# Splitting the last 16 partitions of eight stores over fewer DMA engines, and a SyncE program without a loop, in a batched matmul

## The chip, the cores and the metric

The kernel runs on one core of a Trainium2 chip. The metric is the device time of one execution, in microseconds (us); less is better. The core has the engines TensorE (PE, with its weight loads PEld), VectorE (DVE), ScalarE (ACT), GpSimd (POOL) and SyncE (SP), and 16 DMA engines that move data between the chip's main memory (DRAM) and the on-chip memory (SBUF, 128 partitions). In this kernel SyncE issues all data transfers; its own queue is written SPq in the profile.

## What is computed

```python
b1, b2, m, k, n = 8, 16, 256, 512, 384
# x: (b1, b2, m, k) float32, weight: (b1, b2, k, n) float32
return np.matmul(x, weight).astype(np.float32)
```

These are 128 independent products of a 256x512 by a 512x384 matrix, all in float32 in DRAM. The inputs are 168 MB and the output 50 MB.

## The kernel before

Four matrices form a group (G = 4), so there are NG = 32 groups. In each, a partition holds R = 8 rows of x, of 512 elements (16,384 bytes in a row of memory), and later 8 rows of the output, of 384 elements (12,288 bytes). A group is loaded with one transfer of x and two of the weights, cast to bfloat16, transposed and multiplied on TensorE, copied out of PSUM, and stored with one transfer.

The part of SyncE: loads run LAG = 4 groups ahead of stores. A load waits until the buffer it fills was cast (x_cast, w_cast); a store waits until ScalarE copied the results (o_copied).

```python
def load(e, t, U, s):
    n = t * U + s
    if not isinstance(n, int) or n >= XS:                 # XS = 2 buffers for x
        e.wait_ge(x_cast, n + (1 - XS))
    e.dma_start(x_sb[s % XS][:], x_rows[...]).then_inc(x_in[s % XS], 16)
    for d in range(G // D):                               # two halves of the weights
        slot = (s * (G // D) + d) % WS                    # WS = 4 buffers
        if not isinstance(n, int) or n >= 2:
            e.wait_ge(w_cast, n * (G * S) + ((d + 1) * D * S - 2 * G * S))
        e.dma_start(w_sb[slot][:], w_rows[...]).then_inc(w_in[slot], 16)

def store(e, t, U, s, pieces=1):
    n = t * U + s
    dram = o_rows[bass.ds(n * (G * M), G * M)].rearrange("(p r) n -> p r n", r=R)
    for q in range(pieces):
        rows = slice(q * R // pieces, (q + 1) * R // pieces)
        e.wait_ge(o_copied, n * T + ((q + 1) * T // pieces + BIAS))
        e.dma_start(out=dram[:, rows], in_=out_sb[s % OS][:, rows]).then_inc(
            o_out[s % OS], 16)

@block.sync
def _(e):
    U = OS                                                # OS = 4 output buffers
    for n in range(LAG):
        load(e, 0, NG, n)
    rounds = (NG - LAG) // U
    with e.Fori(0, rounds) as t:
        for s in range(U):
            load(e, t, U, LAG + s)
            store(e, t, U, s)
    for n in range(rounds * U, NG):
        if n + LAG < NG:
            load(e, 0, NG, n + LAG)
        store(e, 0, NG, n, T if n == NG - 1 else 1)       # the last store in T = 4 pieces
    ...                                                   # waits for the last stores
```

The part of ScalarE that a store's completion holds up: before it fills an output buffer again it waits until the store of four groups earlier has landed.

```python
def copy_out(e, t, U, s, q):
    n = t * U + s
    if q == 0:
        e.wait_ge(o_out[s % OS], (t * (U // OS) + s // OS) * 16 + 16)
    e.wait_ge(p_made, n * T + (q + 1 + BIAS))
    e.copy(out=out_sb[s % OS][:, 2 * q : 2 * q + 2, :],
           in_=po[(s * T + q) % PO][:, :, :N]).then_inc(o_copied, 1)
```

Of the kernel before, what the change touches and what calls it, by code (L numbers as in the profile page):

```python
# [11 lines left out]
def kernel(  # L12
# [7 lines left out]
    P = 128  # L20

    b1, b2, M, K = x.shape
    _, _, _, N = weight.shape
    B = b1 * b2
    KO = K // P
# [3 lines left out]
    o_rows = out.rearrange("b1 b2 m n -> (b1 b2 m) n")  # L29
# [9 lines left out]
    G = 4  # L39
    C = P // G  # L40
    R = G * M // P
    T = R // 2
# [3 lines left out]
    NG = B // G  # L46

    XS, WS, OS = 2, 2 * G // D, 4
# [2 lines left out]

    LAG = 4

    ctx.enter_context(tc.tile_critical())  # L54

    def sbuf(name, shape, dtype, n):
        return [
            ctx.enter_context(nc.sbuf_tensor(f"{name}{s}", shape, dtype)) for s in range(n)
        ]
# [6 lines left out]
    def sems(name, n):  # L66
        return [tc.alloc_semaphore(f"{name}{s}") for s in range(n)]
# [9 lines left out]
    out_sb = sbuf("out_sb", [P, R, N], fp32, OS)  # L77
# [6 lines left out]
    id_done, x_cast, w_cast, t_made, t_copied, p_made, o_copied = (  # L84
        sems(name, 1)[0]
        for name in (
            "id_done", "x_cast", "w_cast", "t_made", "t_copied", "p_made", "o_copied"
        )
    )
    x_in, w_in, o_out = sems("x_in", XS), sems("w_in", WS), sems("o_out", OS)  # L90


    BIAS = 8


    def load(e, t, U, s):
        n = t * U + s
        if not isinstance(n, int) or n >= XS:
            e.wait_ge(x_cast, n + (1 - XS))
        e.dma_start(  # L100
            x_sb[s % XS][:],
            x_rows[bass.ds(n * (G * M), G * M)].rearrange("(p r) k -> p r k", r=R),
        ).then_inc(x_in[s % XS], 16)
        for d in range(G // D):
            slot = (s * (G // D) + d) % WS
            if not isinstance(n, int) or n >= 2:
                e.wait_ge(w_cast, n * (G * S) + ((d + 1) * D * S - 2 * G * S))  # L107
            e.dma_start(  # L108
                w_sb[slot][:],
                w_rows[bass.ds(n * (G * K) + d * (D * K), D * K)].rearrange(  # L110
                    "(p k) n -> p k n", k=S * KO
                ),
            ).then_inc(w_in[slot], 16)

    def store(e, t, U, s, pieces=1):
        n = t * U + s
# [5 lines that stand above are left out]
                o_out[s % OS], 16  # L122
            )

    def cast_x(e, t, U, s):
        n = t * U + s
        e.wait_ge(x_in[s % XS], (t * (U // XS) + s // XS) * 16 + 16)
        e.wait_ge(t_made, n * T + ((1 - BS) * T + BIAS))
        for h in range(S):
            ins = e.copy(  # L130
                out=x_bf[s % BS][:, :, h],
                in_=x_sb[s % XS][:].rearrange("p r (q s c) -> p r s q c", s=S, c=KO)[
                    :, :, h
                ],
            )
        ins.then_inc(x_cast, 1)
# [65 lines left out]
    @block.gpsimd  # L202
    def _(e):
        e.memset(identity[:], 0.0).then_inc(id_done, 1)  # L204
        e.wait_ge(id_done, 1)
        make_identity(nc, identity[:], nomemset=True)
        e.drain().then_inc(id_done, 1)

    @block.sync
    def _(e):  # L210
        U = OS
        for n in range(LAG):
            load(e, 0, NG, n)
        rounds = (NG - LAG) // U
        with e.Fori(0, rounds) as t:
            for s in range(U):
                load(e, t, U, LAG + s)
                store(e, t, U, s)
        for n in range(rounds * U, NG):
            if n + LAG < NG:  # L220
                load(e, 0, NG, n + LAG)
            store(e, 0, NG, n, T if n == NG - 1 else 1)
        for s in range(OS):
            e.wait_ge(o_out[s], 16 + 16 * (NG // OS + (T - 1 if s == (NG - 1) % OS else 0)))

    @block.vector
    def _(e):
# [65 lines left out]
```

## Time and profile before

| what | value |
|---|---|
| time, median of 2 runs | 519.82 us (519.78 to 519.85) |
| profiled run | 520.11 us, span in the trace 518.3 us |
| busy: PE, PEld | 315.5 us (61%), 198.8 us (38%) |
| busy: DVE, ACT | 323.9 us (62%), 212.7 us (41%) |
| busy: DMA queue of the data, share of 16 engines | 99.2% |
| bytes read, written | 167.77 MB, 50.33 MB |

A share of busy time says how full an engine is over the whole span, not whether it sets the end. The row of DMA shares in 40 slices says the same by time: each digit is a slice, in tenths. A transfer over 128 partitions is carried out as packets, one for each partition here, spread over the 16 DMA engines; each engine ends its part with a small write of 4 bytes that counts the semaphore up by one. So the trace holds 16 completions for each transfer, and the transfer has landed with the last of them. A packet's record has a start, a duration and a size, but not the number of its DMA engine.

### The profile page before, as it was taken

Reading aid. Unit: us, or ns where it says so; the run is one execution under the profiler, and the core shown is the slowest. Engines: PE = TensorE matmul, PEld = TensorE weight load, DVE = VectorE, ACT = ScalarE, POOL = GpSimd, SP = SyncE. Lnnn points to the kernel's source line nnn. Section 1 sums busy time; section 2 is a strip of 40 time slices with the busy share of each in tenths; the row PEclk is TensorE's granted clock in tenths of the full one; section 3 lists DMA queues with packets and bytes.
Section 4 is the critical chain, followed back from the end, with each engine's and each line's share of the span. In section 5 each row is a group of like instructions: output and inputs, shape, how many; then the busy total and the mean of one; then the engine's idle time right before and its main releaser. Section 6 shows DMA issues by size and latency. Waiting matters only on the chain.

```text
span 518.3 us, 11239 instructions
## 1 busy us (share of the span) xinstructions
PE 315.5 (61%) x4608; PEld 198.8 (38%) x4608; DVE 323.9 (62%) x384; ACT 212.7 (41%) x193; POOL 0.7 (0%) x6
## 2 busy tenths in 40 slices
PE   0686773576655675655756557665567665675653
PEld 0455452343433443433424334343344333443331
DVE  0878867655577555775556765557755577555670
ACT  3065462454234553245542445423454324553242
POOL 0000000000000000000000000000000000000000
PEclk9988788877687778678776877778787868886787
DMA  8999999999999999999999999999999999999995
GB/s 332 431 426 426 427 427 429 430 426 429 430 428 429 431 426 428 428 431 431 425 429 429 430 430 429 427 428 429 430 430 428 426 431 430 429 428 427 428 431 214
DMA packets 18868, 218.16 MB, mean 421 GB/s; under 512 B 2096, under 2 KB 2096, under 8 KB 2608
## 3 DMA queue, kind: packets, MB, share of 16 engines
q1 hardware_dynamic: 18864, 218.11, 99.2%
q8 instruction: 2, 0.03, 0.0%
q14 instruction: 2, 0.02, 0.0%
HBM read 167.77 MB, written 50.33 MB: 421 GB/s over the span
## 4 chain that ended last, share of the span: by engine, by line
DMA 81%; DVE 12%; issue 2%; PE 2%; ACT 1%; SPq 0%; DVEq 0%; ACTq 0%
DMA w_sb<-in_weight_dram 81%; DVE w_bf L148 12%; PE po L181 2%; ACT x_bf L130 0%; DVEq _compat.py:109 0%; SPq L108 0%; ACT out_sb L195 0%; SPq L100 0%; DVE x_t L154 0%; DVEq L143 0%; DVEq L230 0%; SPq L107 0%; ACTq L194 0%; SPq L288 0%; SPq L54 0%
## 5 line engine op out<-in xcount | busy, mean ns | idle before, releaser
L148 DVE CAST w_bf<-w_sb 64x1536 bf16<-64x1536 f32 x256 | 244.5, 955 | 179.4 <-DMA w_sb<-in_weight_dram 166.7
L181 PE MATMUL po<-w_bf,x_t 128*32 128x384 bf16 x4096 | 231.4, 400 | 121.0 <-DVE x_t L154 121.0
L195 ACT COPY out_sb<-po 128x768 f32<-128x768 f32 x128 | 99.2, 802 | 290.2 <-PE po L181 290.2
L181 PEld LDWEIGHTS po<-w_bf,x_t 128*32 128x32 bf16 x4096 | 124.5, 117 | 225.4 <-DVE x_t L154 130.9
L167 PE MATMUL pt<-identity,x_bf 128*128 128x128 f32 x512 | 84.0, 329 | 73.0 <-ACT x_bf L130 73.0
L130 ACT CAST x_bf<-x_sb 128x2048 bf16<-128x2048 f32 x64 | 118.4, 1901 | 6.1 <-DMA x_sb<-in_x_dram 6.1
L167 PEld LDWEIGHTS pt<-identity,x_bf 128*128 128x128 f32 x512 | 74.3, 213 | 84.9 <-issue 84.9
L154 DVE COPY x_t<-pt 128x1024 bf16<-128x1024 bf16 x128 | 79.5, 683 | 1.0
L130 ACT ACT_TABLE_LOAD x1 | 1.3, 1283 | 1.3 <-PEq L237 1.3
masks.py:199 POOL TENSOR_SCALAR_AFFINE_SELECT identity<-identity 128x128 f32<-128x128 f32 x1 | 0.3, 292 | 0.2 <-POOL identity L204 0.2
L204 POOL MEMSET identity<- 128x128 f32 x1 | 0.2, 204 | 0.5 <-SPq L54 0.5
L277 POOL MEMSET const-bfloat16-1.0<- 128x1 bf16 x1 | 0.1, 101 | 0.0
L277 POOL MEMSET const-uint8-127<- 128x1 uint8 x1 | 0.1, 101 | 0.0
L277 POOL MEMSET const-float32-0.0<- 128x1 f32 x1 | 0.1, 98 | 0.2 <-issue 0.2
L277 POOL MEMSET const-float32-1.0<- 128x1 f32 x1 | 0.1, 98 | 0.0
## 6 DMA issues: line engine op xcount, KB each, us to landing
w_sb<-in_weight_dram SPq DMA_DIRECT2D x64, 1536.0 KB, 27.5
x_sb<-in_x_dram SPq DMA_DIRECT2D x32, 2048.0 KB, 25.8
out_dram<-out_sb SPq DMA_DIRECT2D x31, 1536.0 KB, 30.6
out_dram<-out_sb SPq DMA_DIRECT2D x4, 384.0 KB, 3.6
```

The lines of the kernel that those rows point to most:

```text
L130: ins = e.copy(out=x_bf[s % BS][:, :, h], in_=x_sb[s % XS][:].rearrange("p r (q s c) -> p r s q c", s=S, c=KO)[:, :, h],)
L148: e.tensor_copy(out=w_bf[(s * G + d * D + a) % WBS][h * HP : (h + 1) * HP], in_=w_sb[slot][a * HP : (a + 1) * HP, h * KO : (h + 1) * KO, : ...
L154: e.tensor_copy(out=x_t[s % TS][:, 2 * q : 2 * q + 2], in_=pt[(s * T + q) % PT][:].bitcast(bf16),).then_inc(t_copied, 1)
L167: ins = e.transpose(pt[(s * T + q) % PT][:, rr, h, :], words[:, 2 * q + rr, h :: KO // 2], identity[:],)
L181: ins = e.matmul(po[(s * T + q) % PO][mine, rr, :N], x_t[s % TS][:, 2 * q + rr, ko // 2, mine, ko % 2], w_bf[(s * G + i) % WBS][:, ko, :], ...
L195: e.copy(out=out_sb[s % OS][:, 2 * q : 2 * q + 2, :], in_=po[(s * T + q) % PO][:, :, :N],).then_inc(o_copied, 1)
L204: e.memset(identity[:], 0.0).then_inc(id_done, 1)
L277: nc = _bacc.Bacc("TRN2", target_bir_lowering=False, num_devices=1)
```

## The change

SyncE's loop over groups is written out, so that each group can be treated by itself. For eight of the 32 groups (4, 7, 10 ... 25) the store is cut into three transfers: partitions 0 to 111, then k partitions from 112 on, then the 16 - k left. The numbers k are 15, 14 ... 8. The intent is to give the 16 DMA engines unequal numbers of packets: a transfer of k partitions is to use the first k engines, so that the last engines get fewer packets and the first ones more. The three transfers count a semaphore of their own (few); one step later SyncE waits for it and then counts up o_out, for which ScalarE waits.

```diff
+    FEW = {4: 15, 7: 14, 10: 13, 13: 12, 16: 11, 19: 10, 22: 9, 25: 8}
...
+    few = sems("few", 1)[0]
...
+    def store_few(e, n, k):
+        dram = o_rows[n * G * M : (n + 1) * G * M].rearrange("(p r) n -> p r n", r=R)
+        e.wait_ge(o_copied, n * T + (T + BIAS))
+        for a, b in ((0, P - 16), (P - 16, P - 16 + k), (P - 16 + k, P)):
+            e.dma_start(out=dram[a:b], in_=out_sb[n % OS][a:b]).then_inc(few, 16)
...
     @block.sync
     def _(e):
-        U = OS
+        done = [16] * OS
         for n in range(LAG):
             load(e, 0, NG, n)
-        rounds = (NG - LAG) // U
-        with e.Fori(0, rounds) as t:
-            for s in range(U):
-                load(e, t, U, LAG + s)
-                store(e, t, U, s)
-        for n in range(rounds * U, NG):
+        for n in range(NG):
             if n + LAG < NG:
                 load(e, 0, NG, n + LAG)
-            store(e, 0, NG, n, T if n == NG - 1 else 1)
+            if n in FEW:
+                store_few(e, n, FEW[n])
+            else:
+                store(e, 0, NG, n, T if n == NG - 1 else 1)
+            if n - 1 in FEW:
+                e.wait_ge(few, 48 * (1 + list(FEW).index(n - 1)))
+                e.sem_inc(o_out[(n - 1) % OS], 16)
+            done[n % OS] += 16 * T if n == NG - 1 else 16
         for s in range(OS):
-            e.wait_ge(o_out[s], 16 + 16 * (NG // OS + (T - 1 if s == (NG - 1) % OS else 0)))
+            e.wait_ge(o_out[s], done[s])
```

## The prediction

> **What bounds the kernel now.** I read the page's slices and DMA queues first, then the chain that ended last, then SyncE's own waits, and last the single packets of the trace.
>
> ```profile
> DMA  8999999999999999999999999999999999999995
> GB/s 332 431 426 426 427 427 429 430 426 429 430 428 429 431 426 428 428 431 431 425 429 429 430 430 429 427 428 429 430 430 428 426 431 430 429 428 427 428 431 214
> ...
> q1 hardware_dynamic: 18864, 218.11, 99.2%
> ...
> DMA 81%; DVE 12%; issue 2%; PE 2%; ACT 1%; SPq 0%; DVEq 0%; ACTq 0%
> ...
> w_sb<-in_weight_dram SPq DMA_DIRECT2D x64, 1536.0 KB, 27.5
> x_sb<-in_x_dram SPq DMA_DIRECT2D x32, 2048.0 KB, 25.8
> out_dram<-out_sb SPq DMA_DIRECT2D x31, 1536.0 KB, 30.6
> ```
>
> The DMA engines are busy in every slice but the first and last, at a flat 425 to 431 GB/s, and the chain is 81% weight loads. A transfer takes 26 to 31 us from issue to landing, though each engine works on its share of it for only some 4 or 5 us: the queue is always about two groups deep. SyncE's waits show that it is early, not late:
>
> ```profile
> SPq L100 <- ACT x_bf L130: 257.1, 30, 9.4
> SPq L108 <- DVE w_bf L148: 138.1, 58, 3.6
> SPq L121 <- ACT out_sb L195: 36.9, 6, 15.9
> ```
>
> It waits 9 us per group for a buffer of x and 2.4 us for each buffer of weights, with the queue full behind it. So only the work of the DMA engines counts, and of them only the one that ends last.
>
> **The packets.** In mid-run one engine's packet of 12,288 bytes follows the last after about 0.459 us (mean duration 0.462, starts 3 to 4 ns before the end of the one before), and one of 16,384 after 0.608 us. A group gives each engine 8 of x, 16 of weights and 8 of output: 8 x 0.608 + 24 x 0.459 = 15.9 us, and 32 groups make 508 us. That is the kernel; latency at the start and a tail make the rest. Sorting the 16 completions of the last weight load by time, and subtracting the first, gives how far each engine lags behind the fastest (us): 0, 0.28, 0.28, 0.32, 0.32, 0.43, 0.46, 0.53, 0.59, 0.64, 0.65, 0.76, 1.04, 1.93, 2.36, 4.18. Their mean is 0.92. At the first load the largest lag was 0.88. Two engines jump by over 1 us by the fourth load, at 28 and 38 us, where the trace has two packets of instruction fetch of 16,384 bytes (1.06 and 1.11 us). The slowest drifts: its packets take some 3.4 ns more each, and a fetch at 91 us hits it. It ends at 516.3 us of the span; twelve others end near 512.2, for they wait for the last piece of the output, copied at 510.3. So **the ceiling** for any levelling is 4.18 - 0.92 = 3.3 us, 0.6%.
>
> [...]
>
> **The change part by part.**
>
> 1. *Loop to straight code.* It removes register arithmetic and branches from SyncE, which has about 9 us to spare per group: worth 0. It adds code: some 32 x 8 instructions instead of a third of them, at most one or two more fetch packets. Each cost one engine 0.3 to 1.1 us in the trace, and only counts if it hits the engine that ends last: 0 to +0.5 us.
>
> 2. *Packets moved between engines.* An engine has 8 packets in a normal store. In a cut one it has 7 from the 112 partitions, one more if its number is below k, and one more if it is below 16 - k. Summed over k = 15 ... 8, engine 15 loses 8 packets, engine 14 loses 7, ... engine 8 loses 1; engine 0 gains 8, engine 1 gains 7, ... engine 7 gains 1. In time engine 15 loses 8 x 0.459 = 3.7 us and engine 0 gains 3.7. If the drifting engine is 15, as the shape of the change suggests, its lag goes from 4.2 to 0.5. But then engine 0 is last. The fastest engine unhindered would end at 493.3 (its completion of the last weight load) + 4 stores x 8 x 0.459 + 32 small packets x 0.118 = 511.8. With 3.7 more and its own lag of 0 to 1.04 it ends between 515.4 and 516.5, against 516.3 now: -0.9 to +0.2 us. If engine 0 is one of the two that lag by 1.9 and 2.4, +1.1 to +1.5; engine 1 (+3.2 us) and 2 (+2.8) have the same risk, smaller. The ramp moves as much onto one end as it takes off the other: expected **-0.2 us**, not -3.3.
>
> 3. *The new wait on SyncE.* It comes after the next store's issue, and ends when the cut store has landed. Issue to landing is 30.6 us and a step 15.9, so SyncE stands some 14 us, where the next load of x would have been issued after about 9. The load is issued some 6 us late. When the cut store has landed on the last engine, one whole group, 15.9 us of packets less the lag between engines, is still queued behind it; so no engine runs dry: 0. ScalarE needs that buffer only three steps after, so the forwarded count is in time: 0.
>
> 4. *Two more transfers per cut store.* Two more issues of about 0.35 us each on SyncE, hidden, and up to two 4-byte packets of 9 ns per engine: 16 x 9 ns = 0.14 us: +0.1.
>
> 5. *Shared SBUF ports.* This is the part on which I am unsure. [...] It isn't given back: the engines have no idle time. That would be 524 to 532 us.
>
> **Rivals.**
>
> - *Levelling works and the ports don't bind* (4 in 10): parts 1, 2 and 4 alone, about 519.0 to 521.3. For it: the ports' limit is nowhere seen in this trace. Against a larger gain: engine 0.
> - *Port sharing* (6 in 10): 521 to 533. For it: [...] nothing in the queue has slack. Against: the order in which 112 partitions are dealt to 16 engines isn't known to me, and engines that once waited are out of step later and collide less.
> - *SyncE becomes late*, the queue runs dry in each cut step. It would cost several us each time; the depth of the queue and 9 us of waits speak against it. I give it one in twenty, within the second's range.
> - *The last k engines aren't those thought*, and the drifting engine is among those that gain: +0.5 to +3.7 us, thus 520 to 523.5.
>
> **Range and chances.** The two main cases centre on 519.8 and 527; between them I put **523.0 us**. The low end 518.8 is the levelling with a lucky engine 0; the high end 532 is port sharing at its estimate's end. Faster by over 2% (under 509.4) lies below what the packets need, 0.01. Slower by over 2% (over 530.2) needs the upper third of the port case: 0.20. The rest, 0.79, is within 2%.
>
> **What would show it.** The lags of the 16 completions at the last weight load: under levelling alone the largest is 3.5 to 4.5, under port sharing 8 or more, and its jumps stand at the eight cut stores. Packets of 12,288 bytes longer than 0.6 us there, in hundreds, are ports; none means that part 5 fails. SyncE's wait for few should be some 14 us each, with the DMA row still at 9. More instruction fetches would show part 1. I am wrong altogether if the time falls under 518, which would mean that the engines that gain packets had idle time I didn't see, or if it passes 533, which would mean dry queues.

## The result, and the profile after

The changed kernel takes 524.99 us (median of 2 runs, 524.94 to 525.04), the kernel before 519.82: a ratio of 1.010, 95% interval 1.0056 to 1.0143. It is slower by 5.2 us. The forecast was 523.0 with a range of 518.8 to 532.0.

Of the page after, the rows by slice, the packets and queue, the two lines of the chain, and the issues with their time to landing:

```profile
DMA  8999999999999999999999999999999999999994
GB/s 338 429 425 428 425 430 428 427 432 422 401 424 431 421 407 427 430 409 421 429 429 426 430 433 428 426 428 429 424 431 429 431 427 432 428 428 428 427 391 192
DMA packets 18996, 218.16 MB, mean 417 GB/s; under 512 B 2224, under 2 KB 2224, under 8 KB 2736
...
q1 hardware_dynamic: 18992, 218.11, 98.8%
q8 instruction: 2, 0.03, 0.0%
q14 instruction: 2, 0.02, 0.0%
...
DMA 79%; DVE 10%; issue 5%; PE 2%; SPq 1%; ACT 1%; DVEq 0%; ACTq 0%
DMA w_sb<-in_weight_dram 62%; DMA out_dram<-out_sb 18%; DVE w_bf L158 10%; PE po L191 2%; ACT x_bf L140 0%; SPq L123 0%; SPq L103 0%; DVEq _compat.py:109 0%; SPq L111 0%; ACT out_sb L205 0%; DVE x_t L164 0%; DVEq L153 0%; SPq L233 0%; DVEq L242 0%; ACTq L138 0%
...
w_sb<-in_weight_dram SPq DMA_DIRECT2D x64, 1536.0 KB, 27.5
x_sb<-in_x_dram SPq DMA_DIRECT2D x32, 2048.0 KB, 25.5
out_dram<-out_sb SPq DMA_DIRECT2D x23, 1536.0 KB, 30.9
```

The bytes are the same. There are 128 more packets, all small: the semaphore counts of the cut pieces, 16 more per cut store. Each cut store has 32 completions from DMA engines where a whole one has 16: 16 for the first piece, then k and 16 - k. The DMA row is still at 9 everywhere but at the ends. What is new stands in the row below it: three slices fall to 401, 407 and 409 GB/s. A slice is 13.1 us, so these lie at 131 to 144, 183 to 196 and 222 to 235 us, where the first three cut stores (groups 4, 7 and 10), or the loads just behind them, reach the DMA engines. A packet that waits is counted as busy, so the share hides what the rate shows: at 128 to 136 us it is 1.01 before and 1.02 after, at 433 and 403 GB/s. Five stretches of 8 us at places of cut stores, with the columns start and end, length, PE, PEld, DVE, ACT and POOL busy, clock, DMA share and GB/s, first before and then after:

```profile
128.00:136.00 8.00, 3.35 (x28) 2.63 (x32) 7.78 (x10) 2.02 (x3) 0.00 (x0) 0.64 1.01 433
176.00:184.00 8.00, 3.53 (x32) 2.65 (x36) 7.78 (x10) 1.71 (x3) 0.00 (x0) 0.63 1.00 429
224.00:232.00 8.00, 3.71 (x32) 2.83 (x36) 7.78 (x11) 1.59 (x3) 0.00 (x0) 0.61 1.01 431
320.00:328.00 8.00, 3.96 (x32) 2.96 (x36) 7.78 (x11) 1.31 (x2) 0.00 (x0) 0.59 1.01 430
464.00:472.00 8.00, 3.80 (x35) 2.75 (x38) 7.81 (x10) 0.85 (x2) 0.00 (x0) 0.55 1.00 429
```

```profile
128.00:136.00 8.00, 3.68 (x32) 2.82 (x36) 7.78 (x10) 1.71 (x3) 0.00 (x0) 0.62 1.02 403
176.00:184.00 8.00, 3.05 (x40) 2.29 (x28) 7.64 (x8) 3.99 (x4) 0.00 (x0) 1.00 1.00 405
224.00:232.00 8.00, 4.80 (x64) 3.50 (x52) 5.73 (x6) 5.11 (x5) 0.00 (x0) 0.81 1.00 389
320.00:328.00 8.00, 5.85 (x92) 3.90 (x84) 5.04 (x6) 5.80 (x5) 0.00 (x0) 0.93 1.01 424
464.00:472.00 8.00, 5.47 (x92) 3.85 (x84) 5.05 (x6) 5.81 (x5) 0.00 (x0) 0.97 1.02 433
```

The DMA share is 1.00 to 1.02 in all ten lines; the rate falls clearly at the first three cut stores, and hardly at the later two. (The other columns shift because the same clock time meets another point of the group's cycle.)

The single packets say what happens inside. Before, 3 packets of 12,288 bytes after the start took over 0.6 us; after, 105, of which 85 start between 120 and 250 us. At the first cut store the 112-partition part runs almost clean, at 0.46 us a packet with a few of 0.6 to 0.9. Then the 15 partitions come, each on another engine (the store has 16 + 15 + 1 = 32 completions), within 0.2 us, and among these packets stand durations of 0.57, 0.60, 0.83, 1.34, 1.43, 1.80 and 2.24 us.

The completions of the last weight load show what it costs. Before, the fastest engine completes it at 493.33 us of the span, the mean at 494.25 and the slowest at 497.50. After, it is 490.72, 497.04 and 503.02. So the mean engine lost 2.8 us, which no moving of packets between engines can do, and the slowest lost 5.5. The other 2.7 us are uneven sharing. The spread grew from 4.2 to 12.3 us.

SyncE's waits after:

```profile
SPq L103 <- ACT x_bf L140: 182.7, 22, 9.7
SPq L233 <- DMA out_dram<-out_sb: 119.3, 8, 15.9
SPq L111 <- DVE w_bf L158: 115.6, 43, 4.3
SPq L131 <- ACT out_sb L205: 37.3, 6, 16.4
```

The new wait (L233) is 14.9 us for each cut store, as forecast, and the chain now runs 18% through stores. That looks like a culprit, so it was tested.

### The profile page after: what moved, and what is told of

Read it like the earlier page. It is cut to its first block, busy times and chain, and to the rows that moved or that the text cites. A ratio compares the mean times of both kernels' runs of the same rounds, so it can differ in the third digit from the quotient of the medians.

```text
span 523.1 us, 10929 instructions
## 1 busy us (share of the span) xinstructions
PE 314.1 (60%) x4608; PEld 197.3 (38%) x4608; DVE 324.0 (62%) x384; ACT 212.9 (41%) x193; POOL 0.7 (0%) x6
## 4 chain that ended last, share of the span: by engine, by line
DMA 79%; DVE 10%; issue 5%; PE 2%; SPq 1%; ACT 1%; DVEq 0%; ACTq 0%
DMA w_sb<-in_weight_dram 62%; DMA out_dram<-out_sb 18%; DVE w_bf L158 10%; PE po L191 2%; ACT x_bf L140 0%; SPq L123 0%; SPq L103 0%; DVEq _compat.py:109 0%; SPq L111 0%; ACT out_sb L205 0%; DVE x_t L164 0%; DVEq L153 0%; SPq L233 0%; DVEq L242 0%; ACTq L138 0%
## 5 line engine op out<-in xcount | busy, mean ns | idle before, releaser
L177 PE MATMUL pt<-identity,x_bf 128*128 128x128 f32 x512 | 82.9, 326 | 73.9 <-ACT x_bf L140 73.9
```

The costliest lines, as they stand in the source:

```text
L177: ins = e.transpose(pt[(s * T + q) % PT][:, rr, h, :], words[:, 2 * q + rr, h :: KO // 2], identity[:],)
```

## Experiments

The rival causes are named in the first expectation: A, waiting of DMA engines for one another in the small transfers; B, overload of those that gain packets; C, SyncE's new wait; D, the longer SyncE program. Unless its edit says otherwise, each kernel is the changed one with the edit shown. "Long packets" are those of 12,288 bytes over 0.6 us after the start. Times are medians; the kernel before had 519.86, 520.03 and 519.90 us beside the three sets.

| kernel | time, us | ratio to before (95%) | long packets | last weight load: mean, slowest, us |
|---|---|---|---|---|
| before (first run) | 519.82 | | 3 | 494.25, 497.50 |
| after | 524.99 | 1.0056 to 1.0143 | 105 | 497.04, 503.02 |
| straight | 519.98 | 0.9995 to 1.0011 | 2 | 494.22, 497.26 |
| tail16 | 523.90 | 1.0044 to 1.0099 | 151 | 498.71, 502.71 |
| ramp_own | 521.44 | 1.0019 to 1.0042 | 4 | 495.22, 498.97 |
| one120 | 520.62 | 1.0008 to 1.0021 | 58 | 495.73, 498.01 |
| four_own | 519.95 | 0.9984 to 1.0012 | 7 | 495.15, 498.34 |
| four_one | 523.55 | 1.0055 to 1.0084 | 25 | 495.47, 501.79 |
| five_own | 523.06 | 1.0048 to 1.0075 | 6 | 495.23, 500.39 |
| late_wait | 526.04 | 1.0102 to 1.0131 | 123 | 497.57, 504.19 |
| quiet1 | 520.10 | 0.9987 to 1.0015 | 33 | 494.91, 497.24 |
| front1 | 520.21 | 1.0000 to 1.0016 | 52 | 495.11, 497.56 |
| front2 | 520.32 | 1.0003 to 1.0020 | 33 | 494.72, 498.93 |

**The loop alone (straight).**

```diff
-    FEW = {4: 15, 7: 14, 10: 13, 13: 12, 16: 11, 19: 10, 22: 9, 25: 8}
+    FEW = {}
```

> SyncE written out, no store cut. Theories: A, the small transfers over the last 16 partitions make the DMA engines wait for one another; B, the engines that gain packets are simply overloaded; C, SyncE's new wait for a cut store holds up the queue. All three need cut stores, so all expect 519.5 to 520.3 us here. A rival D, that the longer SyncE program costs instruction fetches or issue time, expects most of the 5.2 us, 523 us or more.

519.98 us: the written-out loop is worth nothing either way. Its trace has two fetches of 16,384 bytes and two of 8,192, as many as before. D is out, and everything comes from the cut stores.

**Equal counts, same partitions (tail16).**

```diff
-        for a, b in ((0, P - 16), (P - 16, P - 16 + k), (P - 16 + k, P)):
+        for a, b in ((0, P - 16), (P - 16, P)):
...
-                e.wait_ge(few, 48 * (1 + list(FEW).index(n - 1)))
+                e.wait_ge(few, 32 * (1 + list(FEW).index(n - 1)))
```

> The same eight stores are cut, but in two: 112 partitions and 16, each over all 16 engines, so that every engine has its 8 packets as before. A (waiting for one another on the last 16 partitions) expects about the mean delay of the changed kernel, 2.5 to 3.5 us, thus 522 to 524 us, with packets of 12,288 bytes over 0.6 us at the first cut stores. B (overload by count) expects 519.5 to 520.3. C (SyncE's wait, which stays) expects 523 to 526.

523.9 us, with every engine at 8 packets per store as before. Moving no packet between engines leaves 4.0 of the 5.2 us. The six runs spread from 520.6 to 526.4, far more than the kernel before (519.6 to 520.5): a likely reason, not tested, is that the amount of waiting depends on how the engines happen to stand to one another. In the trace the mean of the last weight load is 4.5 us late, above the 2.5 to 3.5 expected from A and above the 2.8 of the changed kernel. B alone can't be the cause, and C is still open here.

**The same gains without cutting (ramp_own).**

```diff
-    FEW = {4: 15, 7: 14, 10: 13, 13: 12, 16: 11, 19: 10, 22: 9, 25: 8}
+    FEW = {4: 8, 7: 7, 10: 6, 13: 5, 16: 4, 19: 3, 22: 2, 25: 1}
...
-        for a, b in ((0, P - 16), (P - 16, P - 16 + k), (P - 16 + k, P)):
-            e.dma_start(out=dram[a:b], in_=out_sb[n % OS][a:b]).then_inc(few, 16)
+        e.dma_start(out=dram[:], in_=out_sb[n % OS][:]).then_inc(few, 16)
+        later = o_rows[(n + 6) * G * M : (n + 7) * G * M].rearrange("(p r) n -> p r n", r=R)
+        e.dma_start(out=later[0:k], in_=out_sb[n % OS][0 : 4 * k : 4]).then_inc(few, 16)
```

(The wait counts 32 per group, as in tail16.)

> Stores are whole; for the eight groups an extra transfer over k = 8, 7 ... 1 partitions (every fourth partition from 0 on[...]) writes rows that a later store overwrites. So engines 0 to 7 gain 8 to 1 packets as in the changed kernel, and none loses any. B expects that engine 0 ends at 515.4 to 516.5 us of the span if it is one of the twelve fast ones, hence a time of 519.5 to 520.5 us, and 521 to 521.5 if it is one of the two late ones. A expects no long packets. C (the wait stays) expects 523 to 526.

521.44 us, at the upper of the two expectations, with 4 long packets and a mean of the last weight load 0.97 us late; the 36 extra packets alone make 36 x 0.459 / 16 = 1.03. So there are no collisions here, and still 1.6 us are lost. The completions tell who loses them. Engines are counted from 0 in the order in which the small transfers use them. An engine that takes part in the small transfer completes twice, 0.46 us apart. At group 13 (k = 5) the last engine has such a pair, 3.97 and 4.43 us after the first; at group 16 (k = 4) the last, at 4.66, has none. The slow engine is in the first five and not in the first four: it is number 4, not 15. Counted in the same way, engine 0 is 3.7 us behind the fastest after its 8 packets, so it was among the fastest and does not become the last. The time met the range that was given for a late engine 0, but it was another engine that was late.

**Engine 15 alone (one120).**

```diff
+    FEW = {13: 15}
...
+        for a, b in ((0, P - 8), (P - 8, P)):
```

> One store only (group 13) is cut, at partition 120: 120 partitions over 15 engines, 8 packets each, and 8 partitions over 8 engines. The last engine loses all of 8 packets at once, engines 0 to 7 gain one each. If the drifting engine is number 15 and A is right (one store's worth of collisions, about 1 us, instead of eight), the largest lag falls from 4.2 to about 3, and the time to 518.0 to 519.3 us. If the drifting engine has another number, 520 to 521.5 us. B alone, without collisions, expects 517.8 to 518.5 us.

520.62 us, slower than before. After the cut one engine is 3 us ahead of all others: 309.22 us at a load of x where the next is at 312.18. By the 3.67 us of 8 packets, it would have stood at 312.9 otherwise, 1.7 us behind the fastest of the kernel before at this load (311.22). That fits one of the two engines that were late since 28 and 38 us, not the drifting one, which in the kernel before is 3.2 us behind at this load. One store dealt out in 120 partitions made 58 long packets and moved the mean completion by 1.7 us at that load (313.70 against 312.03 before), more than expected.

**Does it matter which partitions are read? (four_own, four_one).** Both add one transfer of 4 partitions to each of eight whole stores, over engines 0 to 3. They differ in one index.

```diff
+    FEW = {n: 4 for n in (4, 7, 10, 13, 16, 19, 22, 25)}
...
+        e.dma_start(out=later[0:k], in_=out_sb[n % OS][0 : 4 * k : 4]).then_inc(few, 16)        # four_own
+        e.dma_start(out=later[0:k], in_=out_sb[n % OS][P - 16 : P - 16 + k]).then_inc(few, 16)  # four_one
```

> Whole stores; in the eight groups an extra transfer over 4 partitions (0, 4, 8, 12[...]) on engines 0 to 3, which are among the early ones; the drifting engine, now taken to be number 4, gets nothing extra. A: no packets over 0.6 us at these places, engines 0 to 3 end 3.7 us later, at or just under the drifting engine: 519.8 to 520.4 us. If the drifting engine were among 0 to 3, 523.5.

> The same, but the 4 partitions are 112 to 115[...]; counts, engines and sizes are the same. A[...]: packets of 12,288 bytes over 0.6 us at the first extra transfers, the last of the four about 1.4 us late there, then fewer as the four have been put out of step; mean landing of the last weight load 0.1 to 0.4 us later[...], time 520.2 to 521.8 us. If the waiting has another cause (the small transfer itself, its DRAM side, the wait on SyncE), the same packets and time[...].

519.95 against 523.55 us. Counts, sizes, engines, waits and the rows written are the same; only the partitions read are 0, 4, 8, 12 or 112, 113, 114, 115. The stretch of the first extra transfer, with columns as above, four_own first:

```profile
128.00:136.00 8.00, 2.82 (x28) 2.33 (x32) 7.78 (x10) 2.69 (x3) 0.00 (x0) 0.95 1.02 433
```

```profile
128.00:136.00 8.00, 3.10 (x28) 2.46 (x32) 7.78 (x10) 2.42 (x3) 0.00 (x0) 0.93 1.01 413
```

With partitions 112 to 115 the packet records have, at 131.42, 131.43, 131.49 and 131.90 us, durations of 0.76, 1.78, 1.89 and 1.24 us, four packets that alone take 0.46. With 0, 4, 8 and 12 the same place has none over 0.6. Four packets of 0.46 us one after another would need 4 x 0.46 = 1.84 us, and the longest is 1.89. So these four packets of a store hold one another up. Where they meet was not shown: a port, as the prediction has it, is the author's assumption of such a place, and no run shows one.

The time was worse than expected for four_one, and the reason is instructive. The mean engine is only 1.2 us late against before, 0.3 more than in four_own and within what was expected, but one engine is 9.0 us behind the fastest at the last weight load, and it has no double completions, so it got no extra packet. Just before the first extra transfer two engines were 2.2 to 2.3 us behind, and it is most likely one of them (an estimate: at 0.46 us a packet, an engine 2.2 us behind is four or five packets behind, and may still be reading its own share when the four early ones arrive); which number it has was not shown. The largest lag at the eight places goes 2.7, 4.1, 5.2, 6.1, 6.8, 7.4, 7.9, 8.3.

**Which engine is slow (five_own).** Four_own with k = 5, so that engine 4 gains 8 packets too, from partition 16.

```diff
+    FEW = {n: 5 for n in (4, 7, 10, 13, 16, 19, 22, 25)}
```

> As with the extra transfers over 4 partitions[...] (519.95 us), but over 5 (0, 4, 8, 12, 16), so that engine 4 gains 8 packets as well[...]. If the drifting engine is number 4, it ends 8 x 0.459 = 3.7 us later: 523.3 to 523.9 us. If it is any other, 519.8 to 520.6.

523.06 us against 519.95. It is a little under the range expected for engine 4, and far from that for any other. One more engine with the same 8 packets costs 3.1 us, while four cost nothing.

**SyncE's wait (late_wait).**

```diff
-            if n - 1 in FEW:
-                e.wait_ge(few, 48 * (1 + list(FEW).index(n - 1)))
-                e.sem_inc(o_out[(n - 1) % OS], 16)
+            if n - 2 in FEW:
+                e.wait_ge(few, 48 * (1 + list(FEW).index(n - 2)))
+                e.sem_inc(o_out[(n - 2) % OS], 16)
```

> The changed kernel, with SyncE's wait for a cut store two steps after it instead of one, when it has long landed. C expects most of the 5.2 us back, 520 to 522 us. A with B expects no difference beyond the spread of the collisions, 524 to 526 us.

526.04 us. Of SyncE's waits in late_wait the line of the new wait, and from its page the two lines of the chain:

```profile
SPq L233 <- DMA out_dram<-out_sb: 0.4, 1, 0.4
```

```profile
DMA 83%; DVE 12%; PE 1%; issue 1%; SPq 0%; DVEq 0%; ACT 0%
DMA w_sb<-in_weight_dram 83%; DVE w_bf L158 12%; PE po L191 1%; DVEq _compat.py:109 0%; SPq L103 0%; SPq L111 0%; ACT out_sb L205 0%; DVEq L153 0%; DVEq L242 0%; SPq L300 0%; SPq L56 0%
```

The wait has fallen from 119.3 to 0.4 us and the stores have left the chain, yet the time is no better; the intervals of the two kernels overlap. Four_own is the reverse: SyncE's wait for these stores is there at full length, as the line of its waits shows, and the time is that of before.

```profile
SPq L234 <- DMA out_dram<-out_sb: 118.3, 8, 15.0
```

C is out. The 18% of stores in the chain was a wait with a full queue behind it.

**Relieving engine 4 (quiet1, front1, front2).** With number 4 known as the last, a small transfer over engines 0 to 3 takes one packet from it per cut store. In these three kernels its four partitions lie four apart, as in four_own.

```diff
+    FEW = {13: 4}                                    # quiet1, front1;  {7: 4, 16: 4} in front2
...
+        pieces = [slice(0, P - 16)] + [slice(P - 16 + r, P, 4) for r in range(4)]   # quiet1
+        pieces = [slice(16, P)] + [slice(r, 16, 4) for r in range(4)]               # front1, front2
+        for a in pieces:
+            e.dma_start(out=dram[a], in_=out_sb[n % OS][a]).then_inc(few, 16)
```

> One store (group 13) as 112 partitions over 16 engines and four transfers of 4 partitions[...] (112, 116, 120, 124 and so on) over engines 0 to 3. Engines 0 to 3 gain 3 packets, every other engine loses one, the drifting one (number 4) among them. A and the identification expect no collisions in the small transfers, an end about 0.46 us earlier: 519.3 to 519.6 us. If the drifting engine isn't 4 but below 4, 521.0 to 521.5.

> One store (group 13) is cut at the front: partitions 16 to 127 over 16 engines, then four transfers of 4 of the first 16 partitions[...], over engines 0 to 3. Engine 4 loses one packet. [...] fewer long packets than with the last 16 partitions (33 over 0.6 us) and 519.4 to 519.8 us; if the 112 partitions collide among themselves, as many, and 519.9 to 520.3 us.

> The same for two stores (groups 7 and 16): engine 4 loses two packets (0.92 us), engines 0 to 3 gain six (2.75 us). Without collisions 519.0 to 519.7 us, bound by engine 4 or 1; with collisions as for one cut, 520.2 to 521.5 us.

None gains: 520.10, 520.21 and 520.32 us. The first misses the 519.3 to 519.6 expected without collisions; the other two lie where collisions were expected. In quiet1 the slowest engine completes the last weight load at 497.24 us, against 497.26 in straight; the 0.46 us taken from engine 4 is not seen in the end. At its cut store there are packets of 0.75 to 0.98 us in the 112-partition part and of 0.72 to 0.91 in the small ones, so a store over 112 partitions makes waiting as well. In front1 the small transfers read the first 16 partitions instead of the last. It has more long packets in all (52 against 33), but fewer at the cut store itself: 4 against 8.

Most of the waiting in these kernels stands elsewhere. What packets took over their usual time, summed over all engines, is 3.5 us at the cut store of quiet1 and 7.9 us after it, and 1.6 and 16.7 us in front1, mostly in weight loads over 128 partitions, from some 12 us after the store on. Four_own, whose stores are whole, has 0.6 us in the same 220 us. At the first cut stores of the changed kernel and of tail16 it was 9.0 and 9.5 us. So with the small pieces over partitions four apart there is less waiting at the store itself (3.5 and 1.6 us against 9.0 and 9.5), but not behind it. No version beats the kernel before.

## Why the prediction was right, and where not

The range held, and the time lies in the case that was given the greater weight, called port sharing, at 521 to 533 us. The parts, one by one:

*Part 1, the loop:* 0 to +0.5 forecast, +0.1 measured (straight), inside its interval of no difference.

*Part 2, the levelling:* the step "if the drifting engine is 15, as the shape of the change suggests" failed. It is number 4 (ramp_own, five_own). So the change gives the last engine 4 packets more (k = 15 to 12 have 16 - k of 4 or less, which leave it out; k = 11 to 8 add one each), instead of 8 fewer. The worth was not -0.2 us but +1.6, which is what ramp_own, with the same 4 packets on engine 4, measured by itself; 4 x 0.459 = 1.8. The fourth rival had named such a case, with +0.5 to +3.7 us. I had taken the purpose of the change for evidence of a fact that the trace before doesn't hold, since its packets have no engine numbers.

*Part 3, the wait:* 14 us forecast and no effect; 14.9 us and no effect.

*Part 4, more transfers:* 128 small packets as counted; no cost apart from the rest was seen.

*Part 5, the ports:* that engines wait for one another at the last 16 partitions was right (four_one against four_own, 523.55 to 519.95 us, and the 105 long packets after); that they do so at ports was not shown. Its size of 4 to 12 us (524 to 532) was the author's estimate, with no trace behind it, and just holds tail16's 4.0. But not all of the 4.0 is what part 5 describes: in tail16 46 us of waiting, summed over engines, stand at the cut stores and 34 in the loads behind them, in the changed kernel 37 and 21. The prediction has no term for the second, so the size was met partly by luck. The waiting was also less even than one size for all eight cut stores allows. The 112 partitions hardly collide in the first cut store (0.46 us a packet, a few of 0.6 to 0.9), though in quiet1 they do (0.75 to 0.98). Summed over the stretch of 19 us from each cut store, what packets took over their usual time, divided by 16 engines, is 1.1, 1.0 and 0.8 us for the first three, then 0.13, 0.15, 0.17, 0.03 and 0.07. That engines which have waited stand apart and meet less is the likely reason, which the prediction named only as an argument against the case. No run tests it, and in tail16 the fall comes later: 0.8 to 1.0 us for each of the first five, then 0.1 to 0.3. The forecast of "hundreds" of long packets fails with this: there were 105.

The two costs of 1.6 and 4.0 us, measured apart, make 5.6; together they were 5.2. That is no exact sum: in the changed kernel the mean engine is 2.8 us late, in tail16 4.5. The point of 523.0 was a mean between two cases, and one term was 1.8 us too low while the other came out at its low end; that it lies only 2.0 us from the result is luck. The range does not depend on it, for tail16 alone, at 523.9, lies within 521 to 533 too.

One announced sign was worked out wrongly. Under levelling alone the largest lag was to be 3.5 to 4.5 us. But a lag is counted from the fastest engine, and engines that lose 7 or 8 packets become faster by 3 us themselves, so levelling alone would have shown some 7 us too. The absolute completions, above all their mean, separate the cases; the lags don't.

**What stays open.** The largest question is the waiting behind the cut stores. In the changed kernel about half of the excess of the first two cut stores (8.9 of 18.0 and 8.1 of 15.3 us, summed over engines) stands some 12 us later, where packets of the weight loads take 0.5 to 1.1 us. All seven kernels that cut stores show it, late_wait without the wait; the four with whole stores and extra small transfers have at most 0.7 us there. No run tells why, and none cuts eight stores with the pieces over partitions four apart, which would part the share of the last 16 partitions from that of the cut itself. Nor was it tried why engine 4 needs some 3.4 ns more per packet (estimated from its lags before), or in which order 112 partitions are dealt to 16 engines.

## What to carry to other kernels

When the DMA engines are full, cutting a transfer into pieces with few partitions can cost more than the balance it buys (4.0 us in tail16): four neighbouring partitions read by four engines held one another up in four_one, where a packet took up to 1.9 us instead of 0.46; and the loads behind a cut store waited too, even where the pieces were spread out (behind it 7.9 us in quiet1 and 16.7 in front1, summed over engines). Read the rate beside the busy share, since a waiting packet is busy, and compare completions by their absolute mean as well as by their spread. Before moving work off the slowest engine, find out which one it is: add a few packets to engines 0 to k - 1 and see from which k on the time moves.

## What the runs showed of the hardware

- The engine that drifts, 4.18 us behind the fastest at the last weight load of the kernel before, is number 4 of the 16, counted from 0 in the order in which small transfers use them (8 packets more on each of the first 4 engines, four_own: 519.95 us; on the first 5, five_own: 523.06).
- Packets of four neighbouring partitions (112 to 115), read by four engines at once, were delayed unevenly in four_one: of four that start within 0.5 us, the durations are 0.76, 1.24, 1.78 and 1.89 us. One engine that gets no extra packet was at most 2.3 us behind before the first such meeting and 9.0 at the last weight load, after eight.
- Two instruction fetches of 16,384 bytes stand at 28 and 38 us, 1.06 and 1.11 us long in the kernel before, 1.07 and 1.11 in the one after. In the kernel before, two DMA engines are late from then on: 1.93 and 2.23 us behind the fastest at 39.8 us, and two still 1.93 and 2.36 behind at the last weight load. With a full queue they did not catch up.
